# First stage of a transformer-block kernel: its instructions ordered by a list schedule, norm weights spread by TensorE, bias rows made in the first stage

## The chip, the cores and the metric

The kernel runs on one core of one Trainium2 chip. A core has five engines, each with its own instruction queue that is worked off in order: PE (TensorE, matrix products), ACT (ScalarE), DVE (VectorE), Pool (GpSimd) and SP, which here only issues transfers (DMAs). ACT and Pool issue transfers too. Engines wait for each other by semaphores. The metric is the device time of one execution in microseconds.

## The reference

One block of a hybrid model on 1024 tokens of width 1024, in float32: a normed input, one wide projection, an mLSTM branch and a sparse-attention (NSA) branch, a gated merge, and a feed-forward part. What the change touches is the first line of it and a table:

```python
u = rms_norm(h, g_norm_mix[l])                  # h: 1024 x 1024
proj = jnp.einsum('btd,de->btw', u, w_in[l]) + b_in[l]
mq, mk, mv, mo, mi, mf, nq, nkv, ngate, merge = split_columns(proj, IN_SIZES)
...
y_m = mlstm_mixer(mq, mk, mv, mo, mi, mf, b_fgate[l], conv_qk[l], g_mlstm_head[l])
y_n = nsa_mixer(nq, nkv, ngate, pe_cmp[l], w_cmp1[l], w_cmp2[l], rel_bias)
# in nsa_mixer: logits + table[..., rel_bucket(distance)], table from rel_bias (32 buckets, 8 heads)
```

## The kernel before

Float32 products are made as three products of a high and a low part (`mm3`, lines 277 to 280; the low part is the source less its high part). The kernel is a chain of stages; each has its own pools of SBUF and PSUM, and the order of the instructions is that of the code (a manual schedule).

*The first stage* (lines 345 to 491) works on eight tiles of 128 tokens. For tile i, `norm(i)` squares the row on ACT, takes the root, corrects it in small operations on DVE (`rstd`) and scales x on DVE by that and by the norm weights `gB`, a 128x1024 tile filled by a broadcast transfer. `trans(i)` transposes the eight 128x128 blocks on PE into PSUM, and `split_evict` writes the high part UTH with ACT and the low part UTL with DVE. `p0(i)` multiplies the tile by 288 columns of w_in (24 products, into value and gate columns), `p0_out(i)` evicts them with a bias; `mv(i)` multiplies it by the 512 columns of the mLSTM's v (24 products) and evicts them into MV. Their weights come as `raw` tiles on SP's queue and are split into p0h/p0l and mvh/mvl by ACT (high) and by DVE or Pool (low, lines 249 to 257). mv lags p0 by two tiles (MVLAG). `keep_busy(n)` issues n products of a zero tile `wz` by itself into an unused bank (line 376). The stage ends with the transpose of the bias rows, `pm` (line 488).

*The second stage* runs two generators against each other (`driver`): a dense one, which makes q, k, o and more from UTH/UTL tile by tile (`fm_tile`, 24 products per half of 512 tokens; weights are asked for two tiles and split one tile ahead), and an auxiliary one with the gates (`gates`) and the mLSTM's chunks (`core`). Between chunks, `core` calls the next of a list of spare steps. These come from `rel_rows` (lines 667 to 680): four times a load of 480 columns of a one-hot table `OH`, a product with `relt` (rel_bias and a row of ones), a DVE copy and a write to `d_row` in DRAM; then eight transfers on Pool's queue that repeat a row of `d_row` on 128 rows, `d_rep` (960 KB each). `relt` and the two `OH` tiles are cleared by DVE at the start of the stage (lines 586 to 593).

`Plan` (lines 64 to 152) is a list scheduler that a later stage of the kernel already uses: a `step` names an engine, a cost in ns, the buffers it reads and writes; `run` repeatedly takes the step that can start soonest, in a time that it keeps itself from these costs, and calls its function, which issues the instructions. It sets only the order in which each engine's instructions stand.

Of the kernel before, what the change touches and what calls it, by code (L numbers as in the profile page):

```python
# [36 lines left out]
MVLAG = 2  # L37
# [5 lines left out]
def cast32(ap):  # L43
    return ap.bitcast(F32)
# [18 lines left out]
class Plan:  # L63
# [95 lines left out]
def body(ctx, tc, a, out, stop=None, dbg=None):  # L159
# [152 lines left out]

# [37 lines left out]
    with ExitStack() as sa:  # L350
# [4 lines left out]
        psT = pa.enter_context(tc.tile_pool(name="psT", bufs=1, space=PSUM))  # L355
        big["p0h"] = ap_.tile([P, KT, 288], F32R, name="p0h", tag="p0h")
        big["p0l"] = ap_.tile([P, KT, 288], F32R, name="p0l")
        big["mvh"] = ap_.tile([P, KT, 512], F32R, name="mvh")
        big["mvl"] = ap_.tile([P, KT, 512], F32R, name="mvl")
# [32 lines left out]

        xs = {}

        def norm(i):
            st = ap_.tile([P, 4], F32, name=f"st{i}", tag="st", bufs=3)
            x_ = xt[i]
            sq = ap_.tile([P, D], mybir.dt.bfloat16, name=f"sq{i}", tag="sq", bufs=1)
            nc.scalar.activation(sq, xt[i], AF.Square, accum_out=st[:, 0:1])
            rstd(st, D)  # L400
            for hf in range(2 if i < 2 else 1):
                ds_ = slice(512 * hf, 512 * hf + 512) if i < 2 else slice(0, D)
                nc.vector.scalar_tensor_tensor(x_[:, ds_], x_[:, ds_], st[:, 2:3], gB[:, ds_], ALU.mult, ALU.mult)
            xs[i] = x_

        def trans(i):
            pt = psT.tile([P, KT, P], F32, name=f"pt{i}", tag="pt", bufs=2)
            for k in range(KT):
                nc.tensor.transpose(pt[:, k, :], xs[i][:, P * k:P * k + P], ident)
            if i + 4 < NT:  # L410
                load_x(i + 4)
            cs = slice(P * i, P * i + P)
            split_evict(UTH[:, :, cs], UTL[:, :, cs], pt)

        p0s = {}

        def p0(i):
            ps = psT.tile([P, 512], F32, name=f"p0_{i}", tag="D", bufs=3)
            cs = slice(P * i, P * i + P)
            for k in range(KT):  # L420
                mm3(ps[:, 0:288], UTH[:, k, cs], UTL[:, k, cs], big["p0h"][:, k, :], big["p0l"][:, k, :], k == 0, k == KT - 1)
            p0s[i] = ps
# [1584 lines left out]
```

## Time and profile before

| | us |
|---|---|
| median of three runs (1587.61 to 1589.59) | 1588.16 |
| profiled execution | 1588.81 |
| its span, first to last instruction | 1587.0 |
| PE busy | 1558.7 (98%) |
| DVE busy | 1046.5 (66%) |
| ACT busy | 743.4 (47%) |
| Pool busy | 211.6 (13%) |

The profile gives times from the span's start. A row of a timeline is start, duration, engine, line of the code, operation, written tile <- read tiles, shape, count, and in brackets the idle time of the engine ahead of it and what ended it. Products overlap: a row's duration is longer than the distance to the next row, and that distance is what a product costs when many follow each other. Rows of several instructions run from the start of the first to the end of the last.

### The profile page before, as it was taken

The numbers are of one execution on the slowest core, as the hardware profiler recorded it, in microseconds if no ns is written. First come the engines' busy times: TensorE is split into PE (matmuls) and PEld (weight loads), VectorE is DVE, ScalarE is ACT, GpSimd is POOL, SyncE is SP. The second block draws the span as 40 slices with busy tenths as digits, with TensorE's granted clock in tenths as the row PEclk, the third lists the DMA queues.
The fourth block names the chain that finished last, engine by engine and source line by source line (L and its number), as shares of the span: only waits on it lengthen the run. The fifth ranks groups of instructions, "written<-read, shape, count | busy, mean of one in ns | idle before, by whom it ended". The sixth has DMA issues, their size and how long they took to land.

```text
span 1587.0 us, 22083 instructions
## 1 busy us (share of the span) xinstructions
PE 1558.7 (98%) x7922; PEld 1320.5 (83%) x7922; DVE 1046.5 (66%) x2226; ACT 743.4 (47%) x1562; POOL 211.6 (13%) x340
## 2 busy tenths in 40 slices
PE   8999999999999999999999999999999999999997
PEld 7877888888999888888887887888888888888886
DVE  6446553246988787840565678666666666979996
ACT  5215455326888687841434343333333333454442
POOL 4012433430113010022002000000000000000130
PEclk9999999999999999999999999999999999999999
DMA  8014532893327332173457214222222223750302
GB/s 254 4 27 102 153 118 88 242 244 109 66 88 125 85 94 68 38 237 107 145 165 248 74 67 146 93 80 80 80 80 80 88 85 115 270 180 33 107 0 107
DMA packets 147262, 181.43 MB, mean 114 GB/s; under 512 B 10302, under 2 KB 104928, under 8 KB 147152
## 3 DMA queue, kind: packets, MB, share of 16 engines
q1 hardware_dynamic: 137312, 157.31, 32.2%
q0 software_dynamic: 9504, 22.13, 5.5%
q8 instruction: 62, 1.02, 0.3%
q10 hardware_dynamic: 336, 0.59, 0.1%
q14 instruction: 48, 0.39, 0.1%
HBM read 137.95 MB, written 49.90 MB: 118 GB/s over the span
## 4 chain that ended last, share of the span: by engine, by line
PE 92%; DVE 4%; DMA 2%; ACT 1%; issue 1%; POOL 0%; DVEq 0%; SPq 0%; POOLq 0%; ACTq 0%
PE PS L280 15%; PE PS L279 15%; PE PS L278 15%; PE d L278 8%; PE d L280 7%; PE d L279 7%; PE T L1088 4%; PE obank L1110 2%; PE obank L1108 2%; PE br L280 2%; PE br L279 2%; PE br L278 2%; PE mv L280 1%; PE mv L278 1%; PE mv L279 1%
## 5 line engine op out<-in xcount | busy, mean ns | idle before, releaser
L278 PE MATMUL d<-UTH,whi 128*128 128x512 f32 x576 | 233.2, 405 | 1.3 <-ACT mg L967 0.7
L280 PE MATMUL d<-UTH,wlo 128*128 128x512 f32 x576 | 225.3, 391 | 0.0
L279 PE MATMUL d<-UTL,whi 128*128 128x512 f32 x576 | 224.7, 390 | 0.0
L1488 DVE TENSOR_TENSOR sl<-PS,sl 128x512 f32<-128x512 f32 x182 | 123.7, 688 | 93.0 <-PE PS L280 90.2
L255 POOL TENSOR_TENSOR wlo<-raw,whi 128x256 fp32r<-128x256 f32 x124 | 94.7, 794 | 318.3 <-ACT whi L249 287.7
L280 PEld LDWEIGHTS d<-UTH,wlo 128*128 128x128 f32 x576 | 108.1, 188 | 23.8
L278 PEld LDWEIGHTS d<-UTH,whi 128*128 128x128 f32 x576 | 108.4, 188 | 19.8 <-ACT mg L967 2.0
L279 PEld LDWEIGHTS d<-UTL,whi 128*128 128x128 f32 x576 | 108.6, 189 | 16.9
L1097 DVE TENSOR_TENSOR TL<-T,TH 128x512 fp32r<-128x512 f32 (+1 forms) x184 | 103.4, 582 | 28.8 <-ACT TH L1093 27.9
L1093 ACT ACTIVATE TH<-T 128x512 fp32r<-128x512 f32 (+1 forms) x184 | 90.3, 511 | 26.4 <-PE T L1088 23.6
L1488 DVE TENSOR_TENSOR sl<-sl,sl 128x512 f32<-128x512 f32 (+1 forms) x116 | 79.1, 688 | 21.3 <-ACT sl L1491 13.3
L1488 POOL TENSOR_TENSOR acc<-acc 128x512 f32<-128x512 f32 x6 | 9.2, 1546 | 622.3 <-DVE acc L1488 622.3
L1491 ACT ACTIVATE sl<-sl 128x512 f32<-128x512 f32 (+1 forms) x85 | 53.6, 632 | 69.0 <-PE PS L279 49.3
L1491 ACT ACTIVATE wh<-sl 128x512 fp32r<-128x512 f32 x61 | 38.5, 631 | 84.0 <-PE PS L279 73.4
L1108 PE MATMUL obank<-TH,VHL 128*128 128x256 f32 x264 | 75.6, 310 | 0.0
L1110 PE MATMUL obank<-TL,VHL 128*128 128x256 f32 x264 | 68.4, 283 | 0.4 <-DVE TL L1097 0.4
L278 PE MATMUL PS<-q 128*128 128x512 f32 x172 | 66.9, 389 | 0.0
L279 PE MATMUL PS<-q 128*128 128x512 f32 x172 | 66.9, 389 | 0.0
L280 PE MATMUL PS<-q 128*128 128x512 f32 x172 | 66.9, 389 | 0.0
L1448 DVE TENSOR_TENSOR q<-br,q 128x512 f32<-128x512 f32 x32 | 21.9, 687 | 66.7 <-ACT q L1436 46.8
L1491 ACT ACTIVATE q<-sl 128x512 fp32r<-128x512 f32 x74 | 43.1, 623 | 42.4 <-PE PS L279 30.3
L1110 PEld LDWEIGHTS obank<-TL,VHL 128*128 128x128 f32 x264 | 50.2, 190 | 1.7 <-DVE TL L1097 0.9
(1284 smaller groups left out, 4243.9 us busy)
## 6 DMA issues: line engine op xcount, KB each, us to landing
raw<-in_w_in SPq DMA_DIRECT2D x40, 512.0 KB, 4.3
ra<-in_w_gate SPq DMA_DIRECT2D x22, 512.0 KB, 3.6
d_gu<-sl SPq DMA_DIRECT2D x44, 256.0 KB, 2.1
q<-d_mg SPq DMA_DIRECT2D x32, 256.0 KB, 3.1
d_rep<-d_row POOLq DMA_DIRECT2D x8, 960.0 KB, 10.2
sl<-in_w_down SPq DMA_DIRECT2D x15, 512.0 KB, 4.3
sl<-d_gu SPq DMA_DIRECT2D x15, 512.0 KB, 5.0
ra<-in_w_up SPq DMA_DIRECT2D x11, 512.0 KB, 3.6
```

What stands on the lines that cost most here:

```text
L255: nc.gpsimd.tensor_tensor(lo[:, zs], v[:, zs], cast32(hi)[:, zs], ALU.subtract)
L278: nc.tensor.matmul(ps, ah, bh, start=first, stop=False)
L279: nc.tensor.matmul(ps, ah, bl, start=False, stop=False)
L280: nc.tensor.matmul(ps, al, bh, start=False, stop=last)
L1088: nc.tensor.transpose(pt[:, z, P * r:P * r + P], e, ident)
L1093: nc.scalar.activation(hl[0][:, 0:m], pt[:, 0:m], AF.Copy)
L1097: nc.vector.tensor_tensor(hl[1][:, 0:m], pt[:, 0:m], cast32(hl[0])[:, 0:m], ALU.subtract)
L1108: nc.tensor.matmul(po, vv, th[:, z, :], start=(st[1] == 0), stop=False)
L1110: nc.tensor.matmul(po, vv, tl[:, z, :], start=False, stop=(st[1] == st[2]))
L1448: nc.vector.tensor_tensor(sg[b], ps, sg[b], ALU.mult)
L1488: return pl.step(alts, lambda e: ENG[e].tensor_tensor(out_(), x(), y(), alu), reads, writes, **kw)
L1491: return pl.step((("ACT", cost),), lambda e: nc.scalar.activation(out_(), x(), fn), reads, writes, **kw)
```

## The change

The first stage is written as steps of a `Plan` with six PSUM banks of one tile `PSA`, and `run` sets the order of its instructions on every engine. Transfers on SP and ACT get a landing time in that plan, counted from their sizes, and at most eight of them are outstanding. The norm weights come as one row of 4 KB (`grow`) and PE spreads them over 128 partitions by two products with a row of ones into two banks `G`, from which DVE reads them. The p0 weights come as three whole transfers into `stage`. `keep_busy` becomes `idle(n)`: n steps of four dummy products. The four bias-row products, their copies (now on ACT) and the `d_row` writes are steps of this stage; `OH` is loaded whole into the space of MV. In the second stage `rel_rows` keeps only the eight `d_rep` transfers, and the clearing of `relt` and `OH` goes.

```diff
@@ class Plan: run
+            st.eng, st.end = e, t + st.alts[e]
             st.fn(e)
-            st.eng, st.end = e, t + st.alts[e]
@@ first stage
-        gB = ap_.tile([P, D], F32, name="gB")
...
-        def keep_busy(n):
-            for _ in range(n):
-                nc.tensor.matmul(pw[:, 0:P], wz, wz, start=True, stop=True)
...
-        nc.scalar.dma_start(gB, a["g_norm_mix"].partition_broadcast(P))
...
-        norm(0)
-        norm(1)
-        keep_busy(20)
-        trans(0)
-        keep_busy(8)
-        ws.split(j_p0[0])
-        ws.split(j_p0[-1], True)
...
+        pA = Plan([PSA[:, n, :] for n in range(2, 8)], ACT=900.0, DVE=1000.0, PE=1000.0, Pool=700.0, SP=700.0)
...
+        def load(eng, kb, parts, reads, writes, cost=450.0, after=0.0):
+            q = {"SP": nc.sync, "ACT": nc.scalar, "Pool": nc.gpsimd}[eng]
+            def go(e):
+                for d_, s_ in parts:
+                    q.dma_start(d_(), s_)
+                n = len(landed)
+                if eng != "Pool":
+                    if n >= 8:
+                        st.end = max(st.end, landed[n - 8][0])
+                    big = [x for x in landed if x[1]]
+                    t = st.end + 2100.0
+                    if kb > 100:
+                        t = max([t] + [x[0] for x in big[-1:]]) + 3.44 * kb
+                    landed.append((t, kb > 100))
...
+        def idle(n):
+            for _ in range(n):
+                b = K()
+                def go(b=b):
+                    for _ in range(4):
+                        nc.tensor.matmul(b.ap[:, 0:P], wz, wz, start=True, stop=True)
+                stp("PE", 400.0, go, (), [b])
...
+        idle(8)
+        def gains():
+            for z in range(2):
+                nc.tensor.matmul(G[:, z, :], ones, grow[:, 512 * z:512 * z + 512], start=True, stop=True)
+        stp("PE", 1600.0, gains, [b_g], [b_G])
+        idle(8)
+        trans(0, norm(0))
+        load_x(3)
+        idle(2)
+        split_p0()
+        p0(0)
+        pA.boost = -2000
+        for z in range(4):
...
+            stp("PE", 1000.0, lambda pb=pb, sl=sl: nc.tensor.matmul(pb.ap[0:NH, 0:480], relt, OH[:, sl], start=True, stop=True), [b_relt, b_oh], [pb], after=13000.0)
+            stp("ACT", 620.0, lambda pb=pb, z=z: nc.scalar.activation(rrow[:, z % 2], pb.ap[0:NH, 0:480], AF.Copy), [pb], [rr])
+            load("Pool", 15, [(lambda sl=sl: d_row[:, sl], rrow[:, z % 2])], [rr], (), cost=560.0)
+        pA.boost = 0
+        trans(1, norm(1))
+        load_x(4)
+        p0(1)
...
+        split_mv(0)
...
+        mv(0)
+        trans(2, norm(2))
+        p0(2)
+        mv(1)
...
+        pA.run()
@@ second stage
-        nc.vector.memset(relt, 0.0)
-        nc.vector.memset(relt[32:33, 0:NH], 1.0)
-        nc.scalar.dma_start(relt[0:32, 0:NH], a["rel_bias"])
...
-            nc.vector.memset(OH[z], 0.0)
...
-            for s in range(4):
-                sl = slice(480 * s, 480 * s + 480)
-                nc.sync.dma_start(OH[s % 2][0:33, :], a["oh"][:, sl])
...
-                nc.tensor.matmul(pb[:, 0:480], relt, OH[s % 2], start=True, stop=True)
...
-                nc.vector.tensor_copy(rrow, pb[0:NH, 0:480])
-                nc.gpsimd.dma_start(d_row[:, sl], rrow)
...
-            spare.extend([lambda: next(rel)] * 12)
+            spare.extend([lambda: next(rel)] * NH)
```

In the changed kernel `split_mv(q)` copies the high part of the q-th pair of row blocks on ACT (`tmvh`) and subtracts on DVE for odd q, on Pool in two pieces for even q (`tmvl`).

On PE, at the start of the program, before (`pw` is the bank of the dummies, `pt` the transposes' bank, x_187 and x_189 tiles 0 and 1, `p_0` p0 of tile 0, whose 24 products follow):

```order
L376 MATMUL pw<-wz 128x128 x20
L409 MATMUL pt_256<-cst,x_187 128x128 x8
L376 MATMUL pw<-wz 128x128 x8
L409 MATMUL pt_294<-cst,x_189 128x128 x8
L376 MATMUL pw<-wz 128x128 x4
L278 MATMUL p_0_339<-p0h,UTH 128x288
L279 MATMUL p_0_339<-p0l,UTH 128x288
```

And of the change (all banks are in `PSA`; MV holds the row of norm weights and the one-hot table here; x_192 and x_224 are tiles 0 and 1; the last two rows begin p0 of tile 1):

```order
L413 MATMUL PSA<-wz 128x128 x32
L568 MATMUL PSA<-MV,ones 128x512 x2
L413 MATMUL PSA<-wz 128x128 x40
L457 MATMUL PSA<-cst,x_192 128x128 x8
L515 MATMUL PSA<-p0h,UTH 128x288 x8
L515 MATMUL PSA<-p0h,UTL 128x288 x8
L515 MATMUL PSA<-p0l,UTH 128x288 x8
L580 MATMUL PSA<-MV,relt 8x480
L457 MATMUL PSA<-cst,x_224 128x128 x4
L580 MATMUL PSA<-MV,relt 8x480
L457 MATMUL PSA<-cst,x_224 128x128 x4
L580 MATMUL PSA<-MV,relt 8x480 x2
```

72 dummies and the two spreading products stand ahead of the first transpose, where 20 dummies stood; the bias-row products stand among the transposes of tile 1.

On ACT, from the eviction of tile 0, before (`raw_193` to `raw_201` are the p0 weights, `sq` the squares of a tile, `st` its statistics):

```order
L274 ACTIVATE UTH<-pt_256 128x8x128
L249 ACTIVATE p0h<-raw_193 128x864
L249 ACTIVATE p0h<-raw_197 128x864
L249 ACTIVATE p0h<-raw_201 128x576
L274 ACTIVATE UTH<-pt_294 128x8x128
L399 ACTIVATE sq_312,st_311<-x_205 128x1024
```

And of the change, from the splitting of the p0 weights (`stage`) on:

```order
L473 ACTIVATE p0h<-stage 128x4x160 x2
L462 ACTIVATE UTH<-PSA 128x4x128 x2
L435 ACTIVATE sq_322,stA<-x_224 128x1024
L492 ACTIVATE tmvh<-rawA_230 128x1024
L438 ACTIVATE stA<-stA 128x1
L492 ACTIVATE tmvh<-rawA_240 128x1024
L530 ACTIVATE VHL<-vt_362 128x4x64
L581 ACTIVATE rrow<-PSA 8x480
L462 ACTIVATE UTH<-PSA 128x4x128
L492 ACTIVATE tmvh<-rawA_249 128x1024
L462 ACTIVATE UTH<-PSA 128x4x128
```

The p0 weights are now split ahead of tile 0's eviction; the square of tile 1 and the first mv splits stand behind it.

On DVE in the same place of the changed kernel, from the statistics of tile 1 on (`vt`, GT and VHL are the p0 eviction of tile 0):

```order
L294 TENSOR_TENSOR stA<-stA 128x1
L443 SCALAR_TENSOR_TENSOR x_224<-x_224,stA,PSA 128x512
L527 TENSOR_TENSOR vt_362<-PSA,BB 128x256
L528 TENSOR_TENSOR GT<-PSA,BB 128x32
L443 SCALAR_TENSOR_TENSOR x_224<-x_224,stA,PSA 128x512
L531 TENSOR_TENSOR VHL<-vt_362,VHL 128x4x64
L498 TENSOR_TENSOR tmvl<-rawA_240,tmvh 128x1024
L463 TENSOR_TENSOR UTL<-PSA,UTH 128x4x128 x2
```

An mv split now stands between the scaling of tile 1 and its UTL.

## Rows read from the trace of the kernel before

**Rows 1.** The view of the cores (span in us, granted clock), and the line of TensorE in the first part of the page (busy us, share of the span, instructions).

```profile
core 0: 1587.0 us, clock 0.997
...
PE 1558.7 (98%) x7922; PEld 1320.5 (83%) x7922; DVE 1046.5 (66%) x2226; ACT 743.4 (47%) x1562; POOL 211.6 (13%) x340
```

**Rows 2.** Whom PE waited for in the first 100 us: engine, line and tile of the waiting instruction, the engine and line waited for, us in total, times, longest.

```profile
PE pt L409 <- DVE x L403: 1.9, 1, 1.9
PE p L278 <- ACT UTH L274: 1.8, 1, 1.8
PE p L279 <- DVE p0l L257: 1.5, 1, 1.5
...
PE p L280 <- DVE UTL L275: 0.7, 1, 0.7
```

**Rows 3.** Timeline of PE, from the first dummy to the start of mv of tile 0 (start us, duration us, engine, line, operation, tiles, shape, count, idle time ahead and what ended it).

```profile
1.08 6.61 PE L376 MATMUL pw<-wz 128*128 128x128 f32 x40 [1.08 <-DVE MV L391]
...
9.62 1.32 PE L409 MATMUL pt<-cst,x 128*128 128x128 f32 x8 [1.93 <-DVE x L403]
...
26.92 0.40 PE L278 MATMUL p<-p0h,UTH 128*128 128x288 f32 x1 [1.82 <-ACT UTH L274]
...
28.18 0.40 PE L280 MATMUL p<-p0h,UTL 128*128 128x288 f32 x1 [0.73 <-DVE UTL L275]
...
29.42 0.44 PE L278 MATMUL p<-p0h,UTH 128*128 128x288 f32 x1
29.66 0.44 PE L279 MATMUL p<-p0l,UTH 128*128 128x288 f32 x1
...
32.73 0.39 PE L278 MATMUL mv<-mvh,UTH 128*128 128x512 f32 x1
```

**Rows 4.** Timeline of PE in the steady part of the first stage, where one tile begins and the next, and at the stage's end.

```profile
52.02 0.39 PE L278 MATMUL mv<-mvh,UTH 128*128 128x512 f32 x1
...
57.59 1.03 PE L409 MATMUL pt<-cst,x 128*128 128x128 f32 x8
58.38 0.38 PE L278 MATMUL p<-p0h,UTH 128*128 128x288 f32 x1
...
61.67 0.39 PE L278 MATMUL mv<-mvh,UTH 128*128 128x512 f32 x1
...
96.81 0.26 PE L488 MATMUL pm<-cst,rows 110*128 110x110 f32 x1
```

**Rows 5.** Busy time of the engines by stretch: from:to, length, then busy us and instructions of PE, PEld, DVE, ACT and POOL, the granted clock of TensorE, DMA share, GB/s.

```profile
0.00:5.00 5.00, 3.92 (x18) 3.92 (x19) 0.29 (x3) 1.89 (x3) 2.03 (x7) 1.00 0.63 211
...
30.00:35.00 5.00, 5.00 (x24) 4.61 (x23) 4.59 (x8) 3.12 (x4) 3.40 (x1) 0.76 0.77 260
```

**Rows 6.** The same timeline of PE cut to a short stretch of the first dummies, and the view of their tile (count, duration ns min/median/max, first and last start).

```profile
5.75 1.50 PE L376 MATMUL pw<-wz 128*128 128x128 f32 x12
...
L376 PE MATMUL pw<-wz x64: 274/275/582, 1.1 to 14.2; 128*128 128x128 f32 x64
```

**Rows 7.** Timeline of PE at one of the four bias-row products in the second stage.

```profile
139.68 0.97 PE L673 MATMUL pb<-OH,relt 128*128 128x480 f32 x2
140.49 0.38 PE L723 MATMUL pn<-MV,PT 128*128 128x129 f32 x2
```

**Rows 8.** Timelines of ACT and of DVE in the first stage (an eviction to UTH, a square with its accumulator read, a split's high part, a root, a scaling of x, the eviction to UTL, the low parts of an mv split and, later, of a single weight split), and from the view of line 255 the Pool's mv splits (count, duration ns min/median/max).

```profile
19.91 0.20 ACT L289 ACTIVATE st<-st 128x1 f32<-128x1 f32 x1 [1.41 <-DVE st L288]
...
24.90 1.06 ACT L249 ACTIVATE mvh<-raw 128x1024 fp32r<-128x1024 f32 x1 [3.29 <-DMA raw<-in_w_in]
25.86 1.01 ACT L274 ACTIVATE UTH<-pt 128x1024 fp32r<-128x1024 f32 x1
...
28.82 1.04 ACT L399 ACTIVATE sq<-x 128x1024 bf16<-128x1024 f32 x1
29.76 0.19 ACT L399 ACTIVATION_READ_ACCUMULATOR sq<-x 128x1 f32 x1
...
20.99 1.28 DVE L403 SCALAR_TENSOR_TENSOR x<-x,st,gB 128x1024 f32<-128x1024 f32 x1
26.90 1.23 DVE L275 TENSOR_TENSOR UTL<-pt,UTH 128x1024 fp32r<-128x1024 f32 x1 [4.63 <-ACT UTH L274]
...
32.61 3.42 DVE L257 TENSOR_TENSOR mvl<-raw,mvh 128x1024 fp32r<-128x1024 f32 x1
...
77.68 1.22 DVE L257 TENSOR_TENSOR wlo<-raw,whi 128x1024 fp32r<-128x1024 f32 x1
...
L255 POOL TENSOR_TENSOR mvl<-raw,mvh x3: 2364/2380/3397, 25.2 to 31.6; 128x1024 fp32r<-128x1024 f32 x3
```

**Rows 9.** Timelines of DVE and PE at the start of the second stage (the clearing of OH; the gate transpose and what it waited for).

```profile
98.49 0.96 DVE L593 MEMSET OH<- 128x480 f32 x2
...
99.54 0.39 PE L611 MATMUL pg<-cst,gif 128*32 128x128 f32 x2 [0.38 <-DVE gif L607]
```

**Rows 10.** Transfers issued from 120 to 180 us (target and source, queue, count, KB each, median us to landing), and the wait of PE in that stretch.

```profile
d_rep<-d_row POOLq DMA_DIRECT2D x4, 960.0 KB, 12.1
raw<-in_w_in SPq DMA_DIRECT2D x5, 512.0 KB, 4.5
...
135.99 0.49 PE L723 MATMUL pn<-MV,PT 128*128 128x129 f32 x2 [1.23 <-DVE PT L717]
```

More of the change, by code (lines that the diff above doesn't have):

```diff
@@ L354, in body @@
         ap_ = pa.enter_context(tc.tile_pool(name="stA", bufs=1, reuse_waits="tile"))
[L355 to L359, printed above, removed]
-        gB = ap_.tile([P, D], F32, name="gB")
+        psT = pa.enter_context(tc.tile_pool(name="psT", bufs=1, space=PSUM, reuse_waits="tile"))
@@ L406, in trans @@
[L406 to L422, printed above, removed]
@@ L481, in body @@
-        ws.split(j_b1["k", 0])
-        p0_out(NT - 1)
-        for i in range(NT - MVLAG, NT):
-            mv(i)
-        pm = psT.tile([P, 512], F32, name="pm", tag="X", bufs=1)
-        nc.tensor.transpose(pm[:, 0:N_ROW], rows, ident[0:N_ROW, 0:N_ROW])
-        nc.vector.tensor_copy(COLS, pm[:, 0:N_ROW])
-        nc.vector.tensor_scalar(NQB, COLS[:, R_NQ:R_NQ + 4], -0.125, None, ALU.mult)
+        rows = ap_.tile([N_ROW, P], F32, name="rows")
+        relt = ap_.tile([33, NH], F32, name="relt")
@@ new lines, in body, with stp @@
+        nc.vector.memset(ones, 1.0)
+        nc.vector.memset(relt, 1.0)
+        pA = Plan([PSA[:, n, :] for n in range(2, 8)], ACT=900.0, DVE=1000.0, PE=1000.0, Pool=700.0, SP=700.0)
+        landed = []
+        DV = (("DVE", 0.0),)
+        def stp(eng, cost, fn, reads=(), writes=(), **kw):
+            return pA.step(((eng, cost),), lambda e: fn(), reads, writes, **kw)
+        def load(eng, kb, parts, reads, writes, cost=450.0, after=0.0):
[12 more added lines that the diff above has]
+                    landed.append((t, kb > 100))
+                    st.lat = t - st.end
+                else:
+                    st.lat = 4500.0
+            st = pA.step(((eng, cost),), go, reads, writes, after=after)
+            return st
@@ new lines, in body, with mk @@
+        K = lambda ap=None, keys=(), make=None, prior=(): pA.buf(keys, ap, prior, make)
+        b_id, b_oh, b_g, b_G, b_relt, b_BV = (K(x) for x in (ident, OH, grow, G, relt, BV))
+        b_BB, b_rows = [K(BB) for _ in range(3)], [K(rows) for _ in range(9)]
+        b_st = [K(stage[:, :, z]) for z in (slice(0, 128), slice(128, 280), slice(280, 288))]
+        xb, ub, sb_ = {}, {}, {}
+        bin_ = a["b_in"]
+        wk = win.rearrange("(k p) c -> p k c", p=P)
+        def load_x(i):
+            def mk(i=i):
+                return ap_.tile([P, D], F32, name=f"x{i}", tag="x", bufs=4)
+            xb[i] = K(keys=[("x", (i + (i > 2)) % 4)], make=mk)
+            load("SP", 512, [(lambda: xb[i].ap, a["x"][P * i:P * i + P, :])], (), [xb[i]])
@@ new lines, in body, with mv_ap, split_mv @@
+        mvt = {}
+        b_mvh, b_mvl = {}, {}
+        def mv_ap(nm, q):
+            if nm not in mvt:
+                mvt[nm] = ap_.tile([P, KT, 512], F32R, name="t" + nm, tag=nm)
+            return mvt[nm][:, 2 * q:2 * q + 2, :]
+        def split_mv(q):
+            h = b_mvh[q] = K(make=lambda: mv_ap("mvh", q))
+            l = b_mvl[q] = K(make=lambda: mv_ap("mvl", q), prior=b_st)
+            r = rawb["mv", q]
+            stp("ACT", 1060.0, lambda: nc.scalar.activation(h.ap, r.ap, AF.Copy), [r], [h])
+            split_low(l, r, h, (("DVE", 1390.0),) if q % 2 else (("Pool", 3400.0),))
@@ new lines, in body, with split_w @@
+        load_x(5)
+        load_x(6)
+        trans(3, norm(3))
+        p0(3)
+        mv(2)
+        load_x(7)
+        trans(4, norm(4))
+        p0(4)
+        whl = {}
+        def split_w(key):
+            r = rawb[key]
+            h = K(make=lambda: wpl.tile([P, KT, P], F32R, name=f"whiA{key[0]}", tag="whi", bufs=2))
+            l = K(make=lambda: wpl.tile([P, KT, P], F32R, name=f"wloA{key[0]}", tag="wlo", bufs=2))
+            stp("ACT", 1060.0, lambda: nc.scalar.activation(h.ap, r.ap, AF.Copy), [r], [h])
+            split_low(l, r, h)
+            whl[key] = h, l
```

249 lines of the change are left out of this document (157 added, 92 removed).

## The prediction

> **What bounds the kernel now.** I read the cores first: one core, a span of 1587.0 us at a granted clock of 0.997 [rows 1]. The page's first part gives TensorE (PE) 98% of that span [rows 1], so time can be won or lost only where PE stands still, runs slowly, or does work that is not the kernel's. The waits of PE come next: nearly all of them in the first 100 us lie in the first stage, where the change is [rows 2]. The timeline of PE then shows what that stage costs. PE starts at 1.08 with 20 dummy products, transposes x0 from 9.62, and reaches the bias-row transpose, which closes the stage, at 96.81 [rows 3, 4]. One token tile costs 9.65 us in the steady part, from 52.02 to 61.67: the 24 products of mv to 57.59, eight transposes, then the 24 of p0 [rows 4]. Eight tiles are 77.2 us. From 9.62 to 96.81 are 87.2 us, so **10.0 us of the stage are lost after the first transpose** (waits, twelve dummies, and a stretch with p0's products 0.24 us apart, where the granted clock averages 0.76 over 30 to 35, partly 1.2 GHz instead of 2.4, after PE had stood for 1.82 and 0.73 us [rows 2, 3, 5]) and 9.62 us before it.
>
> **The change part by part.**
>
> *The dummies, on which the sum turns.* PE now issues 32 dummies, the two products that spread the norm weights, 40 more dummies, and only then x0's transposes. They stand in PE's own queue, so nothing overtakes them. The list books 400 ns for four, 0.1 us each. The trace has the same instruction on the same operand: 20 of them are 40 records, since each float32 product leaves two. They take 6.61 us [rows 3], slowly at first (18 records in the first 5 us, though the clock column says 1.00 there [rows 5]) and then 0.112 us apart, twelve in 1.50 with a last one of 0.27 [rows 6]. A dummy at speed is thus 0.224 us, over twice what is booked.
> The 40 records of before take until 7.69, and a 41st could start at 7.69 - 0.27 + 0.11 = 7.53. Twelve more dummies are 24 records, 2.69 us: 10.22. The spreading products have no row. The nearest is the bias-row product of float32 480 columns, 0.81 us from its start to the next instruction's [rows 7]; 512 columns are 0.86, two 1.73: 11.95. Forty dummies, 80 records, 8.96 us: **x0's transposes start at 20.9, not at 9.62: 11.3 us later.** The bounds on a dummy are 0.1 (the booking) and 0.224; I take the row, as it is the same instruction. No transfer matters for this: x0, the weights and the norm weights are ordered before it, and in the old order x0 was transposed at 9.62 and the last p0 weights were used well before 20.9.
>
> *What the late start buys.* When x0 is transposed, the p0 weights have been split under the dummies, so p0's old waits (1.5 us for p0l, 1.8 for UTH and what follows) have no cause left [rows 2]. What remains hangs on the order of ACT and DVE, because ACT evicts UTH of tile 0 before it squares x1 and before it splits any mv weights. From 20.9, with hops of 0.05 us between engines and 0.2 behind PE:
> - UTH's first half: four transposes 0.4, then 0.51 (half of 1.01) [rows 8]. PE waits about 0.4, and p0 of tile 0 (3.3) and the first bias-row product (0.81) end at about 26.05.
> - x1: ACT is free at 22.35; square 1.13 (28.82 to the end of its accumulator read), the mv split 1.06, root 0.20, then 0.9 of DVE's small operations (1.08 from 19.91 to 20.99, less the root), and half a scaling, 0.64 of the 1.28 [rows 8]. With G in PSUM that half has no row; evictions that read PSUM take 1.23 for 1024 columns [rows 8], so 0.6 to 0.75. x1 is ready at about 26.4: PE waits 0.35.
> - Then transposes and three bias-row products run to 29.6. UTL of tile 1 stands on DVE behind the p0 eviction, the second half of x1 and the mv split of the second pair of row blocks, which starts at 28.0. Alone that split takes 1.22, beside a GpSimd (Pool) one it took 3.42 [rows 8]. Pool has finished its first split by then (24.6 plus 2.4) and cannot begin its second before ACT's copy at 29.3, so I take 1.22: UTL at 29.8, PE waits 0.1. The bound is 3.42, and a wait of 2.2.
> - From there the order puts mv of an earlier tile between the transposes of a tile and its p0, 5.57 us in which ACT and DVE evict; I find no further wait.
>
> The Trainium skill (SBUF — State Buffer, "SBUF: two separate sides") says that a VectorE operation with two SBUF inputs and a GpSimd one that reads SBUF lock each other out for a whole instruction. The GpSimd pieces are now 128x512 instead of 128x1024; by that rule the delay would be one piece, 1.2 to 1.7 us as an estimate from half of 2.38 to 3.40, not 2.2. The sum doesn't use this.
>
> So the stage ends at 20.9 + 77.2 + 4 x 0.81 (bias rows) + 0.85 (waits) = **102.2, 5.4 us later than 96.81**.
>
> *Bias rows moved.* Out of the second stage go four PE products, 4 x 0.81 = 3.24 us on an engine that has no gap there [rows 7]: -3.24. The four DVE copies, four loads and ACT's relt load lie beside PE's work and are worth nothing by themselves.
>
> *The memsets.* DVE clears relt and two OH tiles at the start of that stage, and PE's gate transpose waits 0.38 for the operation behind them [rows 9]. They go: -0.38. DVE reaches it 1.2 us sooner, while PE still has 2.1 us of products ahead of it. Later gate steps stand behind PE's own products and don't gain.
>
> *d_rep.* The eight 960 KB writes take over the four places in Pool's queue that held the small d_row writes, and start some 20 us earlier. Cover: weights (512 KB, 4.5 us to landing) are asked for about a tile (11 us) before they are split, and d_rep landed in 12.1 with four at once [rows 10]. Nothing, if that holds; some 2 to 4 us if a weight comes late. Below nothing: PE's 1.23 us wait for PT [rows 10] could go, as DVE does less.
>
> **Sum**: +5.4 - 3.24 - 0.38 = +1.8. The profiled execution took 1588.81 (1.8 around its span of 1587.0), so 1590.6; the median of the three runs is 0.65 below it, 1588.16, so **1589.9, +0.11%**. About 0.2%, 3.2 us, is what can be told from no change here.
>
> **Rivals.**
> 1. *Tile 1's queue on DVE* (the other side: slower). If Pool's first mv split, which starts when x1's small operations run on DVE, is drawn out to its 3.40 us or more and DVE's split takes 3.42, PE stands 2.2 us before p0 of tile 1. Before, waits of 1.82 and 0.73 were followed by the slower clock: 0.76 over 5 us, 1.2 us lost. Together +2.1 + 1.2 on the forecast: 1593.2, slower. It decides once DVE's split exceeds about 2.6 us. For: the 3.42 row. Against: the order leaves Pool idle between its two splits.
> 2. *The dummies cost what is booked* (faster). At 0.1 us, x0's transposes would start at about 9.8. Weights and splits then set the pace; with 3.5 us of waits the stage would end at 9.8 + 77.2 + 3.24 + 3.5 = 93.7, 3.1 sooner, and the kernel take 1588.16 - 3.1 - 3.6 = 1581.4. Against it stands every dummy record of the trace.
> 3. *d_rep delays a weight* (slower): PE waits 2 to 4 us in the second stage, 1592 to 1594. Against: the load is asked for a tile ahead.
> 4. *All gaps shrink*: no wait in tile 1 and none for PT, -0.85 - 1.23: 1587.8, still no change.
>
> **How the numbers follow.** Forecast and case 4 together 0.65, rival 1 0.19, rival 2 0.07, rival 3 0.09. The range leaves out rival 2 and the far end of 3 and takes in case 4 and rival 1: 1587.0 to 1593.8. Faster: rival 2 and a little more, 0.08. Slower: most of rivals 1 and 3 and a tail of the forecast, 0.27. Same: 0.65.
>
> **What would show it.** In the changed profile x0's first transpose stands at 20.9 (at 10 rival 2 is right); the stage's last mv product ends near 102; PE waits under 1 us in total between 21 and 102, with the clock at 1.00; the second stage is about 3.6 us shorter. A wait of 2 us before p0 of tile 1, or a PE wait on whi between 130 and 180, would make the forecast wrong to the slow side; a first transpose well before 20 would make it wrong to the fast side.

## The result and the profile after

The changed kernel takes **1599.4 us** (median; 1596.5 to 1601.8), beside 1588.9 for the kernel before on the same chip: a ratio of 1.0065, 95% interval 1.0055 to 1.0075. It is 10.5 us slower, where +1.7 us and a range up to 1593.8 were forecast. The profiled execution took 1599.64 us, 9.0 more than the 1590.6 that the prediction's sum gave for one.

The cores and TensorE's (PE's) busy time, which answer to [rows 1], and the waits of PE in the first 125 us, which answer to [rows 2]:

```profile
core 0: 1597.9 us, clock 0.995
...
PE 1573.9 (99%) x8006; PEld 1330.4 (83%) x8006; DVE 1044.9 (65%) x2233; ACT 745.5 (47%) x1575; POOL 209.4 (13%) x347
```

```profile
PE PSA L457 <- DVE x L443: 1.6, 1, 1.6
PE PSA L413 <- DVE wz L359: 1.1, 1, 1.1
PE d L277 <- DVE COLS L638: 0.9, 1, 0.9
PE PSA L515 <- ACT UTH L462: 0.2, 1, 0.2
```

The first stage's four waits of [rows 2], 5.9 us, have become two of 1.8 us together, and PE is busier, 99%; yet the time is longer. The timeline of PE from the first dummy to the first mv product, and around the end of the stage (columns as in [rows 3, 4]), shows where.

```profile
1.09 9.62 PE L413 MATMUL PSA<-wz 128*128 128x128 f32 x64 [1.09 <-DVE wz L359]
10.63 1.98 PE L568 MATMUL PSA<-MV,ones 1*128 1x512 f32 x4
12.54 9.20 PE L413 MATMUL PSA<-wz 128*128 128x128 f32 x80
21.58 1.04 PE L457 MATMUL PSA<-cst,x 128*128 128x128 f32 x8
22.86 1.32 PE L515 MATMUL PSA<-p0h,UTH 128*128 128x288 f32 x8 [0.25 <-ACT UTH L462]
...
26.24 0.97 PE L580 MATMUL PSA<-MV,relt 33*8 33x480 f32 x2
28.79 0.66 PE L457 MATMUL PSA<-cst,x 128*128 128x128 f32 x4 [1.58 <-DVE x L443]
29.37 1.54 PE L580 MATMUL PSA<-MV,relt 33*8 33x480 f32 x2
30.85 1.11 PE L457 MATMUL PSA<-cst,x 128*128 128x128 f32 x4
31.89 3.37 PE L580 MATMUL PSA<-MV,relt 33*8 33x480 f32 x4
...
40.57 0.39 PE L277 MATMUL PSA<-tmvh,UTH 128*128 128x512 f32 x1
...
109.98 0.26 PE L637 MATMUL PSA<-cst,rows 110*128 110x110 f32 x1
111.10 0.50 PE L277 MATMUL d<-UTH,whiAq 128*128 128x512 f32 x1 [0.87 <-DVE COLS L638]
```

A bias-row product, two records, lasts 0.97 us at 26.24 and 1.54 at 29.37; four transposes last 0.66 and then 1.11. The table by stretch (columns as in [rows 5]) has the reason in its granted clock:

```profile
25.00:30.00 5.00, 3.42 (x18) 1.68 (x17) 4.46 (x9) 2.23 (x6) 2.50 (x2) 0.96 0.07 27
30.00:35.00 5.00, 5.00 (x10) 1.08 (x8) 3.13 (x6) 4.39 (x8) 3.03 (x3) 0.50 0.34 108
35.00:40.00 5.00, 5.00 (x21) 4.82 (x21) 1.44 (x5) 2.64 (x6) 4.68 (x10) 0.51 0.41 119
40.00:45.00 5.00, 5.00 (x25) 4.14 (x24) 4.09 (x13) 1.75 (x5) 1.09 (x3) 1.00 0.11 20
```

For nearly 10 us PE runs at half of full speed, 1.2 GHz; before, one stretch of 5 us averaged 0.76 [rows 5], and the one ahead of it 0.90:

```profile
25.00:30.00 5.00, 2.45 (x13) 2.12 (x13) 2.71 (x4) 3.33 (x5) 4.92 (x3) 0.90 0.60 187
```

In the changed kernel PE had stood 1.58 us for x1 before the clock fell. Why x1 was late is seen on VectorE (DVE), of whose five small statistics operations on x1 the last four stand here, with the start of the scaling:

```profile
25.40 0.16 DVE L291 RECIPROCAL stA<-stA 128x1 f32<-128x1 f32 x1 [0.88 <-ACT stA L438]
25.60 1.12 DVE L292 SCALAR_TENSOR_TENSOR stA<-stA 128x1 f32<-128x1 f32 x1
26.76 0.15 DVE L293 TENSOR_SCALAR stA<-stA 128x1 f32<-128x1 f32 x1
26.95 1.00 DVE L294 TENSOR_TENSOR stA<-stA 128x1 f32<-128x1 f32 x1
27.98 0.75 DVE L443 SCALAR_TENSOR_TENSOR x<-x,stA,PSA 128x512 f32<-128x512 f32 x1
```

and, on GpSimd (POOL), the two pieces of its split of the first mv pair:

```profile
25.43 1.28 POOL L504 TENSOR_TENSOR tmvl<-rawA,tmvh 128x512 fp32r<-128x512 f32 x1 [10.63 <-ACT stA L438]
...
26.67 1.25 POOL L504 TENSOR_TENSOR tmvl<-rawA,tmvh 128x512 fp32r<-128x512 f32 x1
```

Operations on 128 numbers last 1.12 and 1.00 us. Both read two SBUF operands, and each ends when a piece of GpSimd's does (26.72 beside 26.71, 27.95 beside 27.92); the two between and ahead, with one tensor operand, take 0.16 and 0.15.

**Two things were thus to be settled**: whether GpSimd makes x1 late, and what brings the clock down. For the second there were three theories. W: it fell because PE stood for x1. A: it fell because the bias-row products use only 33 rows and 8 columns of the array. WA: the wait starts it and the small products keep it down. None of the three will fit every run as it is put here.

### The profile page after: what moved, and what is told of

Read it like the earlier page. It is cut to its first block, busy times and chain, and to the rows that moved or that the text cites. A ratio compares the mean times of both kernels' runs of the same rounds, so it can differ in the third digit from the quotient of the medians.

```text
span 1597.9 us, 22256 instructions
## 1 busy us (share of the span) xinstructions
PE 1573.9 (99%) x8006; PEld 1330.4 (83%) x8006; DVE 1044.9 (65%) x2233; ACT 745.5 (47%) x1575; POOL 209.4 (13%) x347
## 4 chain that ended last, share of the span: by engine, by line
PE 94%; DVE 3%; ACT 1%; issue 1%; DMA 0%; DVEq 0%; ACTq 0%
PE PS L279 15%; PE PS L278 15%; PE PS L277 15%; PE d L277 8%; PE d L279 7%; PE d L278 7%; PE T L1224 4%; PE obank L1246 2%; PE obank L1244 2%; PE br L278 2%; PE br L277 2%; PE br L279 2%; PE PSA L277 1%; PE PSA L279 1%; PE PSA L278 1%; PE PSA L413 1%
## 5 line engine op out<-in xcount | busy, mean ns | idle before, releaser
L277 PE MATMUL d<-UTH,whi 128*128 128x512 f32 x544 | 220.3, 405 | 1.3 <-ACT mg L1103 0.7
L279 PE MATMUL d<-UTH,wlo 128*128 128x512 f32 x544 | 212.8, 391 | 0.0
L278 PE MATMUL d<-UTL,whi 128*128 128x512 f32 x544 | 212.3, 390 | 0.0
L254 POOL TENSOR_TENSOR wlo<-raw,whi 128x256 fp32r<-128x256 f32 x120 | 89.8, 779 | 315.4 <-ACT whi L248 284.9
L279 PEld LDWEIGHTS d<-UTH,wlo 128*128 128x128 f32 x544 | 102.1, 188 | 22.5
L277 PEld LDWEIGHTS d<-UTH,whi 128*128 128x128 f32 x544 | 102.4, 188 | 18.5 <-ACT mg L1103 2.0
L278 PEld LDWEIGHTS d<-UTL,whi 128*128 128x128 f32 x544 | 102.6, 189 | 15.7
L1627 ACT ACTIVATE sl<-sl 128x512 f32<-128x512 f32 (+1 forms) x85 | 53.6, 632 | 69.4 <-PE PS L278 49.4
```

The lines of the kernel that those rows point to most:

```text
L254: nc.gpsimd.tensor_tensor(lo[:, zs], v[:, zs], cast32(hi)[:, zs], ALU.subtract)
L277: nc.tensor.matmul(ps, ah, bh, start=first, stop=False)
L278: nc.tensor.matmul(ps, ah, bl, start=False, stop=False)
L279: nc.tensor.matmul(ps, al, bh, start=False, stop=last)
L1627: return pl.step((("ACT", cost),), lambda e: nc.scalar.activation(out_(), x(), fn), reads, writes, **kw)
```

## The experiments

All are edits of the changed kernel. The kernel before took 1588.9 to 1589.3 us (medians) beside them. The columns: median and range in us, ratio to before with its 95% interval; then, from the profiled execution, the start of x0's transposes, of the first mv product and of the transpose that closes the stage, in us.

| kernel | median (range) | ratio | x0 | mv | end |
|---|---|---|---|---|---|
| changed kernel | 1599.4 (1596.5–1601.8) | 1.0065 (1.0055–1.0075) | 21.58 | 40.57 | 109.98 |
| e1_full | 1594.8 (1594.1–1596.5) | 1.0038 (1.0025–1.0051) | 21.56 | 35.31 | 104.42 |
| e2_nolock | 1599.4 (1597.0–1601.6) | 1.0064 (1.0049–1.0079) | 23.72 | 42.60 | 112.01 |
| e3_few | 1591.2 (1589.1–1593.0) | 1.0013 (1.0003–1.0023) | 10.70 | 32.05 | 101.45 |
| e4_norel | 1599.2 (1598.1–1599.9) | 1.0062 (1.0047–1.0077) | 21.10 | 36.55 | 105.69 |
| e5_lock | 1594.9 (1593.0–1596.5) | 1.0037 (1.0023–1.0052) | 23.47 | 36.12 | 105.60 |
| e6_banks | 1599.5 (1597.9–1599.7) | 1.0064 (1.0049–1.0079) | 23.34 | 40.73 | 110.14 |
| e7_all | 1582.8 (1581.7–1583.3) | 0.9961 (0.9946–0.9975) | 10.70 | 24.44 | 93.57 |
| e8_33x128 | 1599.8 (1598.8–1603.5) | 1.0075 (1.0057–1.0093) | 21.12 | 40.33 | 109.44 |
| e9_128x8 | 1594.1 (1594.0–1597.5) | 1.0038 (1.0023–1.0053) | 23.54 | 37.84 | 106.95 |
| e10_rows | 1594.3 (1593.8–1595.5) | 1.0033 (1.0020–1.0045) | 21.01 | 34.77 | 103.89 |
| e11_all_rows | 1581.8 (1581.1–1583.5) | 0.9953 (0.9935–0.9971) | 13.15 | 25.59 | 94.72 |
| e12_all_norel | 1588.4 (1587.4–1590.1) | 0.9996 (0.9986–1.0005) | 10.68 | 27.02 | 96.13 |

**e1_full: the products on the whole array.**

```diff
-        relt = ap_.tile([33, NH], F32, name="relt")
+        relt = early[:, RW + D:RW + D + P]
-        OH, grow = early[0:33, 0:RW], early[0:1, RW:RW + D]
+        OH, grow = early[:, 0:RW], early[0:1, RW:RW + D]
+        nc.gpsimd.memset(OH, 0.0)
+        nc.vector.memset(relt, 0.0)
+        nc.vector.memset(relt[32:33, 0:NH], 1.0)
...
-    nc.tensor.matmul(pb.ap[0:NH, 0:480], relt, OH[:, sl], ...)
+    nc.tensor.matmul(pb.ap[:, 0:480], relt, OH[:, sl], ...)
```

> The four bias-row products of the first stage use the whole array (a 128x128 stationary block, zeros outside the 33x8 that count, and a 128-row moving block) instead of 33 rows by 8 columns; nothing else moves, so the 1.58 us wait for x1 stays. Theory W (the granted clock fell to 0.50 from 30 to 39.5 us because TensorE stood for x1): clock and time as in the changed kernel, 1599 us. Theory A (it fell because 33x8 products count as little work): no stretch at 0.50, some 5 us less, 1594. Theory WA (the wait makes it fall, the small products keep it down): a stretch at 0.50 of some 4 us instead of 9.5, about 1596.5.

PE's wait for x1 and its clock over 30 to 35 us:

```profile
28.76 0.66 PE L459 MATMUL PSA<-cst,x 128*128 128x128 f32 x4 [1.67 <-DVE x L445]
...
30.00:35.00 5.00, 5.00 (x31) 4.08 (x30) 3.85 (x6) 5.00 (x9) 4.10 (x6) 1.00 0.35 111
```

The wait is as long as in the changed kernel, and the clock stays at 1.00. W, which expected 1599 us here, falls, and so does WA as put, which expected some 4 us at half clock and 1596.5; time and clock are those of A. From x0's transposes to the first mv product are 13.75 us instead of 18.99, so **the half clock cost 5.2 us**, and the kernel is 4.6 us faster. The same number of products with more work in them takes less time.

**e2_nolock: GpSimd's split planned behind x1.** The split of pair 0 gets the scaled x1 as one more thing that it is planned after.

```diff
-    split_low(l, r, h, (("DVE", 1390.0),) if q % 2 else (("Pool", 3400.0),))
+    split_low(l, r, h, ..., hb1[:1] if q == 0 else [])
...
-            pA.step(alts, go, [r, h], [l])
+            pA.step(alts, go, [r, h] + also, [l])
```

> GpSimd's split of the first mv weight pair waits until the first half of x1 is scaled, so that it does not run beside VectorE's small statistics instructions; the bias-row products stay 33x8. If GpSimd's reads are what stretched those instructions, the 1.00 to 1.12 us ones are back near 0.2 us and TensorE's wait for x1 is about 0.35 us instead of 1.58. Theory W and theory WA: the clock then stays at 1.00 and the time falls by 1.2 + 5, to 1593. Theory A: the clock falls all the same, 1598.

Nothing changed, because the edit did not do what it was for. The planner's dependencies order each engine's queue; a wait comes only from data that the instruction really touches. GpSimd has nothing else to do there, so its split started beside DVE's statistics as before (1.12 and 1.00 us again), the wait was 1.58 again and the clock fell. Here it was down (0.71 over 30.5 to 31 us) when PE went on at 30.93, so the products behind the stand did not start the fall. e5 does it with a real dependency.

**e5_lock: a real wait ahead of GpSimd's split.** To e2's edit comes one small operation: GpSimd writes to a statistics column of x1, and so has to wait until DVE has read it for the last time.

```diff
+                    if also:
+                        nc.gpsimd.memset(stA[:, 1, 3:4], 0.0)
                     n = r.ap.shape[1]
```

> A GpSimd memset of the unused fourth statistics column of x1 now stands ahead of GpSimd's split of mv pair 0, so that this split really starts only after VectorE's last read of that column (in e2 only the order on GpSimd was asked for, which held nothing back: the split started at the same place). If GpSimd's reads are what stretched VectorE's 1.12 and 1.00 us statistics instructions, they are at 0.22 and 0.16 here, x1 is scaled 1.7 us sooner and TensorE waits under 0.3 us for it. The 33x8 products stay. If these alone bring the clock down, it falls as before and the time is 1599.4 - 1.6, about 1597.8; if it takes them and the wait together, the clock stays up and the time is about 1592.7.

DVE's two operations, PE around x1, and the clock:

```profile
27.50 0.22 DVE L292 SCALAR_TENSOR_TENSOR stA<-stA 128x1 f32<-128x1 f32 x1
...
27.94 0.16 DVE L294 TENSOR_TENSOR stA<-stA 128x1 f32<-128x1 f32 x1
...
28.15 0.97 PE L582 MATMUL PSA<-MV,relt 33*8 33x480 f32 x2
29.05 0.66 PE L457 MATMUL PSA<-cst,x 128*128 128x128 f32 x4
...
30.00:35.00 5.00, 5.00 (x26) 2.87 (x25) 4.42 (x6) 5.00 (x10) 4.16 (x5) 1.00 0.29 108
```

GpSimd it was: 1.12 and 1.00 us become 0.22 and 0.16, and PE does not wait for x1 at all. And with the products still on 33 rows and 8 columns, the clock stays at 1.00: A falls too. From x0's transposes to the first mv are 12.65 us, 6.3 less than in the changed kernel: 1.6 of wait and 4.7 of clock. (In this execution x0's transposes came 1.9 us later, of which below, so the median gains 4.5 and not 6.3.)

**e8_33x128 and e9_128x8: rows or columns.** Here the wait stays, and only the products' shape changes: few rows and all columns (relt as 33x128), or all rows and few columns. e8 is e1 with relt and OH cut to 33 rows; e9, whose edit of e1 stands here, takes the product to 8 columns:

```diff
-    nc.tensor.matmul(pb.ap[:, 0:480], relt, OH[:, sl], ...)
+    nc.tensor.matmul(pb.ap[0:NH, 0:480], relt[:, 0:NH], OH[:, sl], ...)
```

> The counterpart of e9: the bias-row products have 33 rows and all 128 columns; wait, dummies and all else as in the changed kernel. If it is the few rows that count as little work, the clock falls after the 1.58 us wait as with 33x8 and the time is 1599; if few rows alone don't do it (only few rows and few columns together), the clock stays at 1.00 there and the time is that of e1 and e9, 1594 to 1595.

> The products have 128 rows but 8 columns (stationary block 128x8, zeros below row 33), so that only the columns are few; the rest as in e1. If it is the few rows that count as little work, the clock stays at 1.00 and the time is that of e1, 1594.8; if the few columns suffice, it falls as with 33x8, 1599.4.

The wait and the clock, of e8 and then of e9:

```profile
28.34 0.82 PE L458 MATMUL PSA<-cst,x 128*128 128x128 f32 x4 [1.47 <-DVE x L444]
...
30.00:35.00 5.00, 5.00 (x10) 1.88 (x8) 2.54 (x5) 3.80 (x7) 2.85 (x3) 0.50 0.30 108
```

```profile
30.75 0.66 PE L459 MATMUL PSA<-cst,x 128*128 128x128 f32 x4 [1.56 <-DVE x L445]
...
30.00:35.00 5.00, 4.25 (x17) 1.68 (x18) 4.64 (x9) 3.94 (x8) 2.11 (x3) 1.00 0.19 66
```

With the same stand of about 1.5 us, the clock falls where the products have 33 rows, whatever their columns, and stays where they have 128, even with 8 columns. It is the rows. This rests on more than one profiled execution each, as the mean granted clock is on record for every execution: 0.992 to 0.996 in 17 of the 18 of the changed kernel, e2, e6 and e8, which have both the stand and the 33 rows (0.997 in the other), and 0.997 or 0.998 in all 20 of e1, e5, e9 and e10, which lack one of the two.

**e4_norel: the bias rows back in the second stage**, with the tiles, loads and four products of the kernel before.

> The bias rows are made in the second stage again, as in the kernel before; the first stage keeps the new order, the dummies and the wait for x1, which has no bias-row product ahead of it any more and is some 0.8 us longer. The second stage gets back 3.2 us of products and 0.4 us of waiting, the first stage loses 3.3 us of products. Theory W: the clock falls as before, about 1600. Theory A: no half clock, 1599.4 - 5.1 - 3.3 + 3.6, about 1594.6. Theory WA: half clock for some 4 us after the wait, about 1597.

PE's waits and the clock:

```profile
28.31 0.85 PE L454 MATMUL PSA<-cst,x 128*128 128x128 f32 x4 [2.47 <-DVE x L440]
...
31.99 0.61 PE L279 MATMUL PSA<-p0h,UTL 128*128 128x288 f32 x1 [1.00 <-DVE UTL L460]
...
30.00:35.00 5.00, 4.00 (x17) 3.65 (x16) 4.33 (x10) 4.42 (x8) 4.56 (x9) 0.50 0.40 120
```

There is no bias-row product here, and the clock falls all the same, behind a stand of 2.47 us; the time is about the 1600 that W expected. So none of the three theories holds as put. The reading that fits the runs is that a stand and products on few rows count together: the clock fell behind a stand of about 1.5 us with 33-row products beside it (the changed kernel, e2, e6, e8) and at a stand of 2.47 us or more without them (here, and e11 and e12 below), and it stayed up with a stand of 1.5 to 1.7 us among products on 128 rows (e1, e9, e10) and with 33-row products and no stand (e5). The kernel before kept 1.00 (5 to 15 us) behind a stand of 1.93 us, and lost it behind stands of 1.82 and 0.73 us within 3.1 us [rows 3]. How many rows or how long a stand make the difference was not tried.

The medians give the bias rows' place no worth here (1599.2 beside 1599.4). In the profiled executions the stage ends 4.3 us sooner, and the second stage takes 1490.6 us instead of 1487.9; the medians do not show the 1.5 us that are left.

**e3_few: 20 dummies instead of 72.**

```diff
-                stp("PE", 400.0, go, (), [b])
+                stp("PE", 900.0, go, (), [b])
...
-        idle(8)
+        idle(3)
...
-        idle(8)
+        idle(1)
...
-        idle(2)
+        idle(1)
```

> 20 dummy products on zeros instead of 72 ahead of the first transpose (12, the two gain products, 8), booked at 0.9 us per four instead of 0.4. By the measured 0.224 us per dummy product, the dummies end 11.6 us earlier, at about 10 us, and the x0 transposes start there. The p0 weights are rounded at 11.4 us and their low halves at about 16, the last mv weight lands at about 24, so the first mv starts near 27 or 28 us with some 2 us of waits ahead of it instead of at 40.57: 12 us less, 1587, if the clock is as good as in the changed kernel or better; up to 1591 if the waits bring a longer stretch at half clock.

x0's transposes came at 10.70, 10.9 us sooner, but the first mv only 8.5. DVE again, with PE's wait and the clock:

```profile
16.12 2.92 DVE L292 SCALAR_TENSOR_TENSOR stA<-stA 128x1 f32<-128x1 f32 x1
...
20.26 0.66 PE L457 MATMUL PSA<-cst,x 128*128 128x128 f32 x4 [2.77 <-DVE x L443]
...
25.00:30.00 5.00, 5.00 (x16) 3.39 (x15) 1.99 (x6) 4.21 (x10) 3.55 (x8) 0.50 0.53 188
```

Here the operation lies over both pieces of GpSimd's split (16.52 to 19.01) and takes 2.92 us. The half clock lasts from 21 to 31 us. 8.2 us are won, and the kernel is where the upper end of the expectation was.

**e6_banks: PSUM of the first stage as seven tiles instead of one.**

```diff
-        PSA = psT.tile([P, 8, 512], F32, name="PSA")
+        G = psT.tile([P, 2, 512], F32, name="G")
+        PSB = [psT.tile([P, 512], F32, name=f"ps{n}") for n in range(6)]
```

> PSUM of the first stage as seven tiles (the two gain banks as one, six single banks) instead of one of eight banks, with the same banks in the same order; nothing else. If the second stage's first product waits 0.87 us at 111.1 because the one tile is given up only after its last reader (COLS), it waits under 0.2 us here and the time is 0.7 to 0.9 us less, 1598.6. If it waits for its own bank, or COLS itself, nothing changes.

```profile
110.14 0.26 PE L637 MATMUL ps<-cst,rows 110*128 110x110 f32 x1
110.16 0.48 PE L277 MATMUL d<-UTH,whiAq 128*128 128x512 f32 x1
```

The wait is gone: the second stage's first product follows after 0.02 us instead of 1.12, so the one tile was its cause. The time does not show it (1599.5): from the closing transpose to the end are 1487.6 us, beside 1487.4 to 1488.8 in the kernels that have the wait and the bias rows in the first stage. Of the 1.1 us, 0.6 are given back at 888.5 us, in a wait of PE for DVE (`sl`) that the changed kernel does not have. e7 has one of 0.9 there, but e12, with the same seven tiles, none; what makes it stays open.

**e7_all: e1, e3, e5 and e6 together.**

> All four repairs together: 20 dummies as in e3, products on the whole array as in e1, GpSimd's split held back as in e5, PSUM as in e6. From e3's 1591.2: without its half clock (20.5 to 31 us) 5 us less, without its stretched 2.92 us instruction 1.9 to 2.7 less, without the PSUM wait 0.8 less: 1583, and 1586 if the waits of 1.3 and about 1 us that are left bring the clock down for a while. The first mv then starts at about 25 us.

PE's waits in the first 125 us, without the 1.1 for the first dummy, and the first mv product:

```profile
PE ps L519 <- ACT UTH L464: 0.4, 1, 0.4
PE ps L459 <- DVE x L445: 0.2, 1, 0.2
PE ps L279 <- DVE UTL L465: 0.2, 1, 0.2
...
24.44 0.39 PE L277 MATMUL ps<-tmvh,UTH 128*128 128x512 f32 x1
```

The clock is down only behind the gain products (0.74 over 10 to 15 us), and at 1.00 from 15 us to the stage's end. 1582.8 us as expected, **0.39% faster than the kernel before** (interval 0.25 to 0.54) and 16.6 us faster than the changed kernel. The stage ends at 93.57, 3.2 us sooner than in [rows 4]; the rest is the shorter second stage.

**e12_all_norel: e7 with the bias rows in the second stage.**

> e7 with the bias rows made in the second stage, as in the kernel before. The first stage loses four products (3.2 us) and TensorE waits some 0.8 us longer for x1, the second stage is 2.7 us longer as e4's was against the changed kernel's (1490.6 against 1487.9). Sum +0.3: 1583.1; up to 1585 if the longer wait brings the clock down. If moving the bias rows were worth its 3.2 + 0.4 us, 1586.

5.6 us slower than e7, beyond every time expected. DVE behind x1, PE, and the clock:

```profile
18.41 1.99 DVE L495 TENSOR_TENSOR tmvl<-rawA,tmvh 128x1024 fp32r<-128x1024 f32 x1
20.32 1.49 DVE L530 TENSOR_TENSOR VHL<-vt,VHL 128x256 fp32r<-128x256 f32 x1
...
22.46 0.41 PE L279 MATMUL ps<-p0h,UTL 128*128 128x288 f32 x1 [3.00 <-DVE UTL L460]
...
20.00:25.00 5.00, 2.54 (x12) 2.54 (x13) 4.86 (x11) 3.69 (x7) 5.00 (x7) 0.81 0.34 114
```

Without the products' 3.2 us PE catches up with DVE, whose queue is drawn out by GpSimd's four pieces (16.81 to 22.95): PE stands 3.00 us for UTL and the clock is at 0.5 again from about 23 to 26 us. The first mv comes 2.6 us later although four products fewer stand ahead of it, and the second stage is 2.0 us longer. In this pair the new place of the bias rows is worth more than their products: they are work for PE while DVE gets ready. The planner also orders the rest anew without them (GpSimd's four pieces follow each other here, in e7 they come two and two), so the 5.6 us are the difference of two orders and not the price of the products alone.

**e10_rows and e11_all_rows: the gain products on all rows** (e10 is e1 with this, e11 is e7 with it).

```diff
-        ones = ap_.tile([1, P], F32, name="ones")
+        ones = ap_.tile([P, P], F32, name="ones")
-        ... early[0:1, RW:RW + D]
+        ... early[:, RW:RW + D]
+        nc.vector.memset(grow, 0.0)
```

> e1 with the two gain products on all 128 rows as well (stationary block of ones 128x128, the gains in row 0 of a moving block whose other rows are zero), so that no product of the first stage has few rows. The 72 dummies and the wait for x1 stay. If the stretch at half clock that e2, e5, e6 and e9 show from about 14 to 17 us, behind the 1x128 gain products, comes from their one row, no execution has it: the second dummy block takes 9.2 us and not 10.8, all runs lie close together at the lower end of e1, about 1594.1. If it has another cause, the runs scatter from 1594.1 to 1596.5 as in e1.

> e7 with the gain products on all 128 rows. In e7 the clock is at 0.50 from about 9 to 12.3 us, and the x0 transposes take 1.91 us instead of 1.04. If that comes from the gain products' one row, the clock stays at 1.00, the transposes end some 0.9 us sooner, and as the p0 weights are rounded at about 12.5 us the gain is 0.3 to 0.9: 1582.2. Otherwise 1582.8 as e7.

In e2, e5, e6 and e9, and also in e3, e7 and e12, the clock was down for some 3 us after the 1x128 gain products, at 0.50 from 14 to 16 us in the first four, without any stand of PE; in the changed kernel, e1, e4 and e8, which have the same products, it was not. The second dummy block, of e9 and of e10:

```profile
12.88 10.83 PE L415 MATMUL PSA<-wz 128*128 128x128 f32 x80
```

```profile
12.08 9.09 PE L416 MATMUL PSA<-wz 128*128 128x128 f32 x80
```

That is 1.6 to 1.7 us where it happens, most of why x0's transposes start at 21.0 to 21.6 in some executions and at 23.3 to 23.7 in others. e10 has no such stretch and its runs lie a little closer (1.7 us against 2.4 in e1), but one profiled execution without it does not prove the rows to be the cause, as e1's had none either. The mean granted clock says a little more: 0.998 in all six executions of e10, and 0.997 in seven of the 14 of e1, e5 and e9. That speaks for the one row without proving it. e11 cannot be told from e7 (1581.8 beside 1582.8, ranges overlap): the load of the gains is issued only at 2.28 instead of 0.91, behind VectorE's memset, and PE stands 2.48 us ahead of the gain products, probably for that load (the profile names a DVE operation whose result they do not read). The clock falls in that stand instead: 0.50 over 8 to 10 us.

## Why the prediction failed, point by point

The step that failed is **"From 20.9, with hops": the wait for x1 and what follows it**, and with it the clock. Two of its terms were wrong: "0.9 of DVE's small operations", which took 2.6 us, and "the clock at 1.00", which was 0.50 for nearly 10 us and cost 5.2. Set against the profiled execution (1599.64 instead of 1590.6, 9.0 us):

- *Dummies.* Forecast 20.9 for x0's transposes, measured 21.58: +0.7. The mechanism and its price of 0.224 us were right (80 records in 9.2 us after the gains); rival 2 is out. Of the 0.7, 0.4 lie in the first 32 dummies and 0.2 in the gain products, 1.91 us instead of 1.73. e3 agrees from the other side: 52 fewer dummies, 10.9 us, where 52 times 0.224 are 11.6; the clock was down there (0.74 over 5 to 10 us).
- *x1.* Forecast wait 0.35, measured 1.58: +1.2. The term "0.9 of DVE's small operations" came from a stretch of the old timeline where they ran free; beside GpSimd's split they took 2.6. The old trace had a hint of it: at 17.70 us the second of these operations took 0.41 us instead of 0.22 and ended with a split of GpSimd's (18.11 beside 18.09). The prediction saw that GpSimd's first split lies on them (rival 1 says so) but priced it for DVE's large split, which then took the 1.22 us assumed. e5 shows that this is the cause. The Trainium skill (SBUF — State Buffer, "SBUF: two separate sides") has this rule: a VectorE operation with two SBUF inputs and a GpSimd one that reads SBUF share a pair of ports, and whichever starts first has it for its whole instruction. The prediction weighed it at the large operation only. The changed kernel's trace agrees to 0.03 us at the ends of the pieces. e3's fits less well: there VectorE's operation starts 0.40 us ahead of the first piece (16.12 and 16.52) and still ends with the second.
- *Clock.* Forecast "with the clock at 1.00"; measured 0.50 for nearly 10 us. From x0's transposes to the first mv, 12.25 us were forecast (two tiles' transposes and p0 at 8.16, 3.24, 0.85) and 18.99 measured: +6.7, of which 1.2 are x1's wait and 5.2 the clock (e1). This is **the largest part of the miss**. Rival 1 had a stand of PE and the clock, but another stand, for tile 1's UTL behind DVE's large split, and gave 1593.2. It took the clock's price, 1.2 us, from one stretch of the old trace, 30 to 35 us; the stretch ahead of it, at 0.90, is part of the same fall, which makes 1.7. And dense products on 128 rows followed the stand there; here products on 33 rows stood on both sides of it.
- *Steady tiles.* Forecast 69.0 from the first mv to the stage's end, measured 69.4: +0.4.
- *Second stage.* Forecast 3.6 shorter, measured 2.3 (1487.9 beside 1490.2): +1.3. The gate transpose's wait went, as forecast. A wait that the prediction did not name, 0.87 us for PSUM's one tile at the start of that stage, came instead; e6 shows its cause, though not that it is what makes the 1.3. The wait for PT went from 1.8 to 1.4 us in all.
- *d_rep* (rival 3): no wait of PE for a weight came up (from 112 to 200 us it waits for PT alone); out.

The sum 0.7 + 6.7 + 0.4 + 1.3 is 9.1 of the 9.0 us.

## What to carry to other kernels

When an order moves small operations beside a long one of GpSimd, price every operation on the path that has two SBUF operands as ending no sooner than GpSimd's instruction, however small it is itself: 0.2 us became 1.1, and 2.9 over two pieces. Where PE will have to wait, look at what the clock will do, not only at the idle time: here a stand of 1.6 us among products on 33 rows cost 5.2 us more, and filling those products with zero rows gave that time back. An order that a planner writes is no wait: whether an instruction really waits must be seen in the trace.

## What the runs showed of the hardware

- Products on 33 rows do not do for TensorE's clock what products on 128 rows do, zeros or not: with the same stand of about 1.5 us the granted clock was 0.50 over 30 to 35 us with 33x8 and 33x128, and 1.00 with 128x8 and 128x128. The Trainium skill (TensorE: Matmul & The Clock Gate, Part 1) has the gate follow how busy TensorE has been; by busy time alone, e1 and the changed kernel (3.33 and 3.42 us busy from 25 to 30 us) would have had the same clock. The measurement decides.
- Products on one row (1x128 stationary, 1x512 moving) were followed by about 3 us of lowered clock in seven of the eleven profiled executions that have them, though PE never stood still there. That the one row is the cause is not proved.
- A VectorE operation on 128x1 numbers with two SBUF operands ends only with the GpSimd instruction beside it (1.12 and 1.00 us instead of 0.22 and 0.16), and in e3 only with the second of two in a row (2.92).
